# A decoder layer on eight cores: leaner opening loads, a later store of Q, two pairs of PSUM banks at the end of attention, and LayerNorm and up weights moved apart

## The chip, the cores and the metric

The kernel runs on the 8 cores of one Trainium2 chip, cores 0 to 3 on one die and 4 to 7 on the other. Every core computes 2048 of the 16384 tokens, and no core waits for another. The metric is the device time of the slowest core in microseconds (us).

Executions come in two states. In the fast one the cores have a granted TensorE clock of about 0.99. In the slow one a die, sometimes both, falls to between 0.81 and 0.98 and its cores take up to 19% longer.

## The reference, cut to what matters

```python
def token_mixer(x, w_in, b_in, sinks, g_mix_a, g_mix_b, w_out):
    proj = jnp.einsum('bsd,de->bse', x, w_in) + b_in
    # ... split into qa, ka, va (8 heads of 128) and qb, kb, vb (16 query heads of 64, 2 kv heads)
    qa = rope(qa, pos); ka = rope(ka, pos)
    ya = dilated_mixture_attention(qa, ka, va)     # patterns (128,1), (512,4), (2048,16)
    # ... rope on qb, kb
    yb = sink_window_attention(qb, kb, vb, sinks)
    y = jnp.concatenate([rms_norm(ya, g_mix_a), rms_norm(yb, g_mix_b)], axis=-1)
    return jnp.einsum('bse,ed->bsd', y, w_out)

def swiglu(x, w_up, w_down):
    gate, up = jnp.split(jnp.einsum('bsd,df->bsf', x, w_up), 2, axis=-1)
    return jnp.einsum('bsf,fd->bsd', jax.nn.silu(gate) * up, w_down)

x = layer_norm(ALPHA * x + token_mixer(...), ln1_g, ln1_b)
x = layer_norm(ALPHA * x + swiglu(x, w_up, w_down), ln2_g, ln2_b)
# D_MODEL 2048, SEQ 16384, D_FF 5632, group A 8 heads, group B 16 heads
```

## The kernel before

The large matmuls are bf16; a few small ones, for sums over partitions, are float32. Each core goes through these stages: V and K of its tokens and of the 2048 before them; Q and group B's attention; group A's attention; the output projection; LayerNorm 1 (LN1); and the feed-forward in two halves of 1024 tokens (`st` 0 and 1), with LN2 in the second half's shade. TensorE is fed by the other engines, and each engine's operations come in the order in which the program lists them for it (a case where that costs 1.1 us is shown below: an exponential behind a Square). The scheduling helpers `S_.pe`, `S_.act`, `S_.dve` and `S_.pool` record an operation with what it reads and what it writes. In the views of the profile PE is TensorE and PEld its weight loads; `arena` is the kernel's whole SBUF (the on-chip memory) and `sp` its PSUM (where TensorE writes its sums), used as eight banks.

The opening loads x and the V weights in turn, and the second token tile waits for the whole of its x:

```python
    for p_ in (1, 1, 2, 4, 4, 4):                      # x of the first tile and wv, in turn
        ...
        S_.dma("pool", wv[:, q_, :], k.wv_d[q_], ...)  # [128, 1152]: 1024 columns of A, 128 of B
    S_.dma("sp", bv, k.bv_d[0], [], [bbv], "bv")       # V's bias, already spread over 128 partitions
    load_x(1, (4, 4, 4, 4))
    ...
    load_ra(0); load_ra(1)                             # rotary tables
    # first tile: 8 matmuls (4 blocks x 2 banks) as each chunk lands; then
    for blk in range(4):
        v_tile(1, blk)                                 # waits for bx[1] + bwv, all chunks
```

Group A runs in 32 units (8 heads, 4 residues `c`), each with three patterns: S matmuls, an exponential on ScalarE (ACT), a mask on VectorE (DVE), and PV matmuls into one pair of banks, `ob` and `lb`. At the end of a unit the pair is evacuated. Until unit 25 each unit also computes a Q projection; `dveq` holds its rotary operations, of which the last, the add at L331, stores Q.

```python
    for u in range(32):
        for p_ in range(3):
            ... spend.append(a_S(hn, cn, pats[pn], nb % 2))   # S, exponential, mask of a later pattern
            run(dveq, 2 if p_ == 0 else 1)
            if p_ == 2:
                proj(u + 32 + LEAD, 0)
            a_PV(h, c, pats[p_], spend.pop(0), p_ == 0, p_ == 2)
        a_evac(h, c)

    def a_evac(h, c):
        S_.act(... Ln of lb ...); S_.act(... Exp ...)
        S_.dve(... yc = ob * ls ...)                   # L879: frees the banks
        S_.act(... sq = Square(yc) ...)                # L887, for group A's RMS norm
        S_.pool(... y = copy of yc ...)                # reordered, then stored when the head is done
        S_.pool(... acc += sq ...)
        if c == 3 and h < 7:
            S_.dma("sp", k.ys_d[h], y, ...)            # store of a head of y
```

y goes through HBM. Its loads for the output projection are issued from one queue, in this order: 14 for the first half, 14 for the second half, and then, in unit 28, head 6 of both halves, whose store has just been put into the same queue.

```python
    for c in KCB: y_load(0, c)
    for c in KCA[:6]: y_load(0, c)
    for c in KCB + KCA[:6]: y_load(1, c)
    ...
        if u == 28:
            k.y_load(0, 6); k.y_load(1, 6)
```

LN1 has its mean and inverse deviation in SBUF, and its sums on GpSimd (POOL):

```python
    def ln1_tile(st, n, hh, z, bz):
        S_.dve(... z = z - mu ...)                     # L1139
        S_.dve(... z = z * rs ...)                     # L1140
        S_.act(... x1b = z * g + b ...)
        S_.dma("act", k.x1s_d[n, :, c0:c0 + 512], z, ...)     # the residual, stored in HBM
    # the output projection's second half works these off as it goes:
        for _ in range(2 if si % 2 else 1):
            if jobs:
                jobs.pop(0)()
```

The softmax here doesn't subtract the row's maximum and nothing guards it: scores larger than these inputs give would overflow.

Of the kernel before, what the change touches and what calls it, by code (L numbers as in the profile page):

```python
# [203 lines left out]
def build(debug=False):  # L204
    nc = bass.Bass("TRN2", target_bir_lowering=False)
    dt = nc.dram_tensor
    k = K()
    k.nc = nc
    ein = lambda n, s: dt(n, s, F32, kind="ExternalInput").ap()
    k.xT_d = ein("xT", [8, 128, KC, 512])  # L210
    k.xres_d = ein("xres", [KC, 128, TOK])
    k.ropeA_d = ein("ropeA", [8, 128, 2, 512])
    k.ropeB_d = ein("ropeB", [4, 128, 2, 512])
    k.ropeBh_d = ein("ropeBh", [128, 2, 128])
    k.maskA1_d = ein("maskA1", [128, 4, 64])
    k.mask_d = ein("mask", [128, 3, 256])
    k.onh_d = ein("onh", [128, 128])
    k.perm_d = ein("perm", [128, 128])
    k.wv_d = ein("wv", [KC, 128, VW])
    k.wk_d = ein("wk", [8, 128, KC, 128])  # L220
    k.wkb_d = ein("wkb", [128, KC, 128])
    k.wq_d = ein("wq", [16, 128, KC, 128])
    k.bqk_d = ein("bqk", [128, 25])
    k.bsw_d = ein("bsw", [128, 16])
    k.bv_d = ein("bv", [2, 128, VW])
    k.wout_d = ein("wout", [KC, 128, KC, 128])
    k.wup_d = ein("wup", [FC, 128, KC, 256])
    k.wdn_d = ein("wdn", [KC, 128, FC, 128])
    k.gmix_d = ein("gmix", [128, KC])
    k.lnp_d = ein("lnp", [128, 4, KC])  # L230
    k.sinks_d = ein("sinks", [128, 8])
    k.outT_d = dt("outT", [KC, 128, TOK], F32, kind="ExternalOutput").ap()
    k.ka_d = dt("ka", [8, 8, 128, 512], BF16, kind="Internal").ap()
    k.kb_d = dt("kb", [128, NKB * 128], BF16, kind="Internal").ap()
    k.vs_d = dt("vs", [2 * TOK, VW], BF16, kind="Internal").ap()
    k.ys_d = dt("ys", [KC, 128, TOK], BF16, kind="Internal").ap()
    k.rb_d = dt("rb", [128, TOK], F32, kind="Internal").ap()
    k.wdb_d = dt("wdb", [KC, 128, FC, 128], BF16, kind="Internal").ap()
    k.x1s_d = dt("x1s", [KC, 128, TOK], F32, kind="Internal").ap()
    k.z2s_d = dt("z2s", [KC, 128, TOK], F32, kind="Internal").ap()  # L240

    stack = ExitStack()
    with stack:
        k.S = Sched(nc, stack)
        k.arena = stack.enter_context(nc.sbuf_tensor("arena", [128, ARENA_EL], BF16))
        k.SP = [stack.enter_context(nc.psum_tensor("sp%d" % i, [128, 1024], F32)) for i in range(4)]
        k.bBK = [Buf("bk%d" % i) for i in range(8)]
        persist(k)
        phase1(k)
        phase2(k)  # L250
        final = phase3(k)
        k.S.emit(final)
    return nc
# [30 lines left out]
def persist(k):  # L284
# [15 lines left out]
    S_.dma("pool", k.perm, k.perm_d, [], [k.bperm], "perm")  # L300
# [53 lines left out]
def phase1(k):  # L354
# [48 lines left out]

    s0 = xs[slot_of[0]]
    bl0 = []
    kc = 0
    for p_ in (1, 1, 2, 4, 4, 4):
        o_ = XO + kc * 1024
        b_ = S_.buf("x0_%d" % kc, o_, o_ + p_ * 1024)
        S_.dma("pool", s0[:, kc:kc + p_, :], k.xT_d[0, :, kc:kc + p_, :], [], [b_], "x0_%d" % kc)  # L410
        bl0 += [b_] * p_
        for q in range(kc, kc + p_, 2):
            n_ = min(2, kc + p_ - q)
            for q_ in range(q, q + n_):
                S_.dma("pool", wv[:, q_, :], k.wv_d[q_], [], [bwv[q_]], "wv%d" % q_)
        kc += p_
    bx[0] = bl0
    S_.dma("sp", bv, k.bv_d[0], [], [bbv], "bv")
# [6 lines left out]
    S_.dma("pool", wkb, k.wkb_d, [], [bwkb], "wkb")  # L425
    k.bvs, k.bka, k.bkb = [], [[] for _ in range(8)], []
# [5 lines left out]

    def v_out(t, blk, groups, banks):
        vi = nx("vo", 2)
        vo, bvo = VO[vi]
        w = 0
        for gi, (c0, c1) in enumerate(groups):
            bk = banks[gi]
            args = dict(out=vo[:, c0:c1], in0=bank(k, bk)[:, 0:c1 - c0], in1=bv[:, c0:c1], op=ALU.add)
            S_.dve(lambda args=args: nc.vector.tensor_tensor(**args), [k.bBK[bk], bbv],  # L440
                   [bvo] if gi == 0 else [], [] if gi == 0 else [bvo])
            w = c1
        b = Buf("vs%d_%d" % (t, blk))
        r0 = t * 512 + blk * 128
        S_.dma("sp", k.vs_d[r0:r0 + 128, 0:w], vo[:, 0:w], [bvo], [b], "vo%d" % vi)
        k.bvs.append(b)

    def v_tile(t, blk):
# [3 lines left out]
        for (c0, c1) in groups:  # L452
            bk = nx("bk", 8)
            banks.append(bk)

            def mm(bk=bk, c0=c0, c1=c1):
                for kc in range(KC):
                    ins = nc.tensor.matmul(bank(k, bk)[:, 0:c1 - c0], x[:, kc, blk * 128:blk * 128 + 128], wv[:, kc, c0:c1],  # L458
                                           start=(kc == 0), stop=(kc == KC - 1))
                return ins  # L460
            S_.pe(mm, bx[t] + bwv, [k.bBK[bk]])
        v_out(t, blk, groups, banks)

    def k_tile(t, h):
# [11 lines left out]
        ko, bko = KO[ki := nx("ko", 3)]  # L476
# [32 lines left out]
    load_ra(0)  # L509
    load_ra(1)  # L510
# [9 lines left out]
    for blk in range(4):  # L520
        v_out(0, blk, [(0, 512), (512, 1024)], [blk * 2, blk * 2 + 1])
    for blk in range(4):
        v_tile(1, blk)
# [37 lines left out]
def phase2(k):  # L561
# [33 lines left out]
    VA = [PW("vA0", 69 * 128), None]  # L595
# [17 lines left out]
    def load_kv(h):  # L613
        if h == 1:
            P2 = Place(k, o_b, 2 * ARENA_EL)
            KA[1] = P2("kA1", 8 * 512)
            VA[1] = P2("vA1", 69 * 128)
# [6 lines left out]
        first = [True]  # L624

        def ld(out, in_):
            S_.dma("sp", out, in_, k.bvs, [bv_] if first[0] else [], "va%d" % (h % 2), joins=[] if first[0] else [bv_])
            first[0] = False
        own = k.vs_d[TOK - 128:2 * TOK, col]
        ld(vt[:, 0:17, :], own.rearrange("(b p) d -> p b d", p=128))  # L630
        own2 = k.vs_d[TOK - 512:2 * TOK, col].rearrange("(j i c) d -> c i j d", c=4, i=128)
        for c in range(4):
            ld(vt[:, 17 + 5 * c:22 + 5 * c, :], own2[c])
        v3 = k.vs_d[:, col].rearrange("(f m r) d -> f m r d", f=2, r=16)
        for f in range(2):
            ld(vt[:, 37 + 16 * f:53 + 16 * f, :], v3[f])
# [198 lines left out]

    def a_PV(h, c, pat, pb, first, last):
        p = pb[0]
        vt, bv_ = VA[h % 2]
# [31 lines left out]
        S_.pe(mm, [pb[1], bv_, k.bones, k.bonh], [bOB, bLB])  # L870

    k.y7 = None

    def a_evac(h, c):
        ls, bls = LS[nx("ls", 2)]
# [8 lines left out]
        if h == 0:  # L884
            S_.pool(lambda: nc.gpsimd.tensor_tensor(out=ac, in0=yc, in1=yc, op=ALU.mult), [byc], [bacc[c]])
        else:
            S_.act(lambda: nc.scalar.activation(out=sq, in_=yc, func=AF.Square), [byc], [SQ[1]])  # L887
# [9 lines left out]
        if h > 0:  # L897
            eng, ve = ("dve", nc.vector) if (h, c) == (7, 3) else ("pool", nc.gpsimd)
            S_._add(eng, lambda: ve.tensor_tensor(out=ac, in0=ac, in1=sq, op=ALU.add), [SQ[1], bacc[c]], [bacc[c]])
        if c == 3 and h < 7:  # L900
# [6 lines left out]
    def reduce_a(c):  # L907

        bk = 6 + nx("pj", 2)
        if c == 3:  # L910
            bk = 4
# [41 lines left out]
    for u in range(32):  # L953
# [11 lines left out]
        for p_ in range(3):  # L965
# [4 lines left out]
            run(dveq, 2 if p_ == 0 else 1)  # L970
# [3 lines left out]
            if 28 <= u < 31:  # L974
                for _ in range(2):
                    if len(k.norms) > 48:
                        out_norm(k, *k.norms.pop(0))
            if u >= 29 and p_ == 1:
                reduce_a(u - 29)
        if u == 0:  # L980
            reduce_b(3)
        a_evac(h, c)
        proj(u + 32 + LEAD, 1)
    for i, (n, hh) in enumerate(OUT_PRE):
        out_mm(k, 0, n, hh, OUT_BK[i], KCB, True, False)
        if i == 2:
            reduce_a(3)
# [94 lines left out]
def phase3(k):  # L1082
# [53 lines left out]
    def ln1_tile(st, n, hh, z, bz):  # L1136

        (mu, bmu), (rs, brs) = stat[hh]
        S_.dve(lambda: nc.vector.tensor_tensor(out=z, in0=z, in1=mu, op=ALU.subtract), [bz, bmu], [bz])  # L1139
# [19 lines left out]

    for st in range(2):  # L1160
# [7 lines left out]

        def load_xr(si):
            if si < len(steps):  # L1170
                n, hh = steps[si]
                c0 = st * TS + hh * 512
                S_.dma("sp", xr[si % 4][0], k.xres_d[n, :, c0:c0 + 512], [], [xr[si % 4][1]], "xr")
        for si in range(3):
            load_xr(si)
        for si, (n, hh) in enumerate(steps):
            bk = OUT_BK[si % 6]
            load_xr(si + 3)
            xb, bxb = xr[si % 4]
# [9 lines left out]
            if si == 0:  # L1189
                while fins:  # L1190
                    fins.pop(0)()
# [5 lines left out]
            stats(n, hh, z, bz, sqs)  # L1197
            for _ in range(2 if si % 2 else 1):
                if jobs:
# [11 lines left out]
    wdone(k, "xr")  # L1211
    def ln2_tile(st, n, hh, idx):
        c0 = st * TS + hh * 512
        (mu, bmu), (rs, brs) = stat[hh]
        if st == 0:
            z, bz = slot("zl%d" % idx, R[0] + (4 + idx % 6) * 2048)
            S_.dma("sp", z, k.z2s_d[n, :, c0:c0 + 512], [bz2s[(n, hh)]], [bz], "zl%d" % (idx % 6))
# [52 lines left out]
    for st in range(2):  # L1270
        h = [None] * FC
        bh = [None] * FC
        order = [(0, 0), (1, 0), (0, 1), (1, 1)] + [(f, hh) for f in range(2, FC) for hh in range(2)]
        wcur = {}
        sg = [slot("sg%d_%d" % (st, i), misc(8 + i)) for i in range(2)]
        for ui, (f, hh) in enumerate(order):
# [22 lines left out]
            if ui == 0:  # L1299
                while fins:  # L1300
                    fins.pop(0)()
            for _ in range(2):
                if jobs:
# [5 lines left out]
        for si, (n, hh) in enumerate(steps):  # L1309
            wkey = ("d", st, n, hh if st else 0)  # L1310
            w, bw = k.wts[wkey]
            bk = si % 4
# [76 lines left out]
def prepare_inputs(x, w_in, b_in, sinks, g_mix_a, g_mix_b, w_out, ln1_g, ln1_b, w_up, w_down, ln2_g, ln2_b):  # L1389
# [13 lines left out]
    wv = con(np.concatenate([w_in[:, 2048:3072], w_in[:, 4224:4352]], 1).reshape(KC, 128, VW))  # L1403
# [22 lines left out]
    shared = dict(wq=wq, wk=wk, wkb=wkb, wv=wv, bqk=bqk, bsw=bsw, wout=wout, wup=wup, wdn=wdn, gmix=gmix, lnp=lnp,  # L1426
# [35 lines left out]
```

## Time and profile before

The median was 3120.53 us (3116.96 to 3122.29 fast, one slow at 3255.28).

The page's first part gives busy time, share of the span and instructions of each engine on the slowest core, core 4:

```profile
PE 2981.2 (96%) x15993; PEld 1425.5 (46%) x15993; DVE 1089.1 (35%) x1440; ACT 645.8 (21%) x891; POOL 608.3 (20%) x592
```

TensorE is busy 2981.2 of 3112.1 us. What can be won is its idle time of 131 us, and the slow clock after pauses: by the trace's records of the granted clock this core's TensorE was busy for 35.8 us at a clock of 0.50, the tail left out. The view of waits says what ended TensorE's pauses on core 4. Each line names the waiting instruction, what it waited for, the sum in us, how often, and the longest.

```profile
PE sp L849 <- DVE arena L879: 32.5, 26, 5.4
PE sp L516 <- DMA arena<-wv: 23.9, 7, 9.3
PE sp L458 <- DMA arena<-xT: 11.6, 1, 11.6
PE sp L1288 <- DMA arena<-wup: 6.0, 1, 6.0
...
PE sp L1076 <- DVE arena L1065: 2.5, 1, 2.5
```

The first line is PV waiting for the evacuation of the one pair of banks; the next two are the opening. The fourth is the first up weights (over all cores the waits for up weights are 4.7 us in the mean), and the last is the output projection waiting for the norm of y (L1065).

The timeline of TensorE in the opening (columns: start, duration, engine, line, operation, count; in brackets the idle time before and what ended it) shows the slow start (8 matmuls in 3.57 us, where K's first 15 take 3.40), the second tile's wait, and K's start at 96.82:

```profile
9.35 3.57 PE L516 MATMUL sp<-arena 128*128 128x512 bf16 x8 [9.35 <-DMA arena<-wv]
...
67.58 29.41 PE L458 MATMUL sp<-arena 128*128 128x512 bf16 x128 [11.60 <-DMA arena<-xT]
96.82 3.40 PE L471 MATMUL sp<-arena 128*128 128x512 bf16 x15
```

One end of a unit in group A, in the timeline of core 4:

```profile
809.48 1.04 DVE L331 TENSOR_TENSOR arena<-arena 128x512 bf16<-128x512 f32 x1
810.06 0.64 PE L824 MATMUL sp<-arena 128*128 128x64 bf16 x17
810.45 0.67 DVE L879 TENSOR_TENSOR arena<-sp,arena 128x512 bf16<-128x512 f32 x1
...
811.27 0.63 ACT L887 ACTIVATE arena<-arena 128x512 f32<-128x512 bf16 x1 [1.37 <-DVE arena L879]
811.81 2.12 ACT L829 ACTIVATE arena<-sp 128x1024 bf16<-128x1024 f32 x2
```

The evacuation (L879) begins as Q's store (L331) ends. Two lines further on the next exponential (L829) starts at 811.81; its scores were ready at 810.70 (S, L824: 810.06 plus 0.64).

LN1's two operations between 1095 and 1230 us, in the view of groups (busy us and mean ns of one; then idle before and what ended it):

```profile
L1140 DVE TENSOR_TENSOR arena<-arena 128x512 f32<-128x512 f32 x32 | 53.7, 1678 | 3.5 <-DVE arena L1139 0.2 <-ACT arena L1115 0.2
L1139 DVE TENSOR_TENSOR arena<-arena 128x512 f32<-128x512 f32 x32 | 26.2, 818 | 0.0
```

Both have two inputs in SBUF, and beside POOL's sums they slow down. Over all cores, the 160 of the first half's 256 multiplies (L1140) that began while a sum ran took 1.57 to 2.95 us, 2.25 in the mean; the other 96 took 0.69 to 0.91. The subtractions (L1139) took 1.12 us in the mean when they began during a sum (80 of them) and 0.68 otherwise. The residual add of the output projection (L1195), which has one input in PSUM, took 681 ns in the same stretch, and no more than 0.69 us where it began during a sum (1080 to 1260 us, all cores).

### The profile page before, as it was taken

The numbers are of one execution on the slowest core, as the hardware profiler recorded it, in microseconds if no ns is written. First come the engines' busy times: TensorE is split into PE (matmuls) and PEld (weight loads), VectorE is DVE, ScalarE is ACT, GpSimd is POOL, SyncE is SP. The second block draws the span as 40 slices with busy tenths as digits, with TensorE's granted clock in tenths as the row PEclk, the third lists the DMA queues.
The fourth block names the chain that finished last, engine by engine and source line by source line (L and its number), as shares of the span: only waits on it lengthen the run. The fifth ranks groups of instructions, "written<-read, shape, count | busy, mean of one in ns | idle before, by whom it ended". The sixth has DMA issues, their size and how long they took to land.

```text
span 3112.1 us, 40181 instructions; the slowest of 8 cores (3099.8 to 3112.1 us)
## 1 busy us (share of the span) xinstructions
PE 2981.2 (96%) x15993; PEld 1425.5 (46%) x15993; DVE 1089.1 (35%) x1440; ACT 645.8 (21%) x891; POOL 608.3 (20%) x592
## 2 busy tenths in 40 slices
PE   5999999998997998999999999999999999999996
PEld 2445554545664443444444444444444444444443
DVE  0555555787776776420010000001421000100123
ACT  0000000665555133320000001111320000001223
POOL 2000000452322877000000002222000000002234
PEclk9999999999999999999999999999999999999998
DMA  9852213155548798754434447888864344335554
GB/s 175 160 125 81 78 52 80 42 125 120 127 111 208 148 192 173 150 118 80 80 70 82 76 98 187 211 205 196 206 148 82 70 80 79 70 102 185 180 207 166
DMA packets 191032, 398.48 MB, mean 128 GB/s; under 512 B 86912, under 2 KB 104576, under 8 KB 169856
## 3 DMA queue, kind: packets, MB, share of 16 engines
q0 software_dynamic: 29232, 167.06, 31.2%
q1 hardware_dynamic: 144912, 198.44, 21.4%
q10 hardware_dynamic: 16704, 30.42, 2.7%
q8 instruction: 128, 2.10, 0.3%
q14 instruction: 56, 0.46, 0.1%
HBM read 471.11 MB, written 91.82 MB: 181 GB/s over the span
## 4 chain that ended last, share of the span: by engine, by line
PE 75%; DMA 11%; DVE 7%; issue 3%; ACT 3%; POOL 1%; another core or an unknown queue 0%; SPq 0%; DVEq 0%; ACTq 0%; POOLq 0%
PE sp L1288 37%; PE sp L1322 10%; PE sp L471 7%; DMA arena<-x1s 7%; PE sp L458 7%; PE sp L695 5%; PE sp L1076 4%; DMA arena<-wv 1%; DVE arena L658 1%; DMA arena<-z2s 1%; DVE arena L1140 1%; ACT arena L1317 1%; DVE arena L1333 1%; DVE arena L879 1%; ACT arena L829 1%
## 5 line engine op out<-in xcount | busy, mean ns | idle before, releaser
L1288 PE MATMUL sp<-arena 128*128 128x512 bf16 x5632 | 1220.4, 380 | 10.4 <-DMA arena<-wup 6.0
L1288 PEld LDWEIGHTS sp<-arena 128*128 128x128 bf16 x5632 | 552.0, 98 | 679.7 <-issue 18.5
L1322 PE MATMUL sp<-arena 128*128 128x512 bf16 x2816 | 608.3, 379 | 2.2 <-ACT arena L1295 2.2
L1296 DVE TENSOR_TENSOR arena<-sp,arena 128x512 bf16<-128x512 f32 x176 | 121.6, 692 | 983.9 <-ACT arena L1295 983.9
L1322 PEld LDWEIGHTS sp<-arena 128*128 128x128 bf16 x2816 | 275.4, 98 | 335.3 <-issue 3.7
L1295 ACT ACTIVATE arena<-sp 128x512 f32<-128x512 f32 x176 | 105.1, 598 | 928.0 <-PE sp L1288 919.9
L127 POOL DMA_DIRECT2D arena<-wup x88 | 46.7, 530 | 1102.7 <-PE sp L1288 1071.1
L1116 POOL TENSOR_TENSOR arena<-arena 128x512 f32<-128x512 f32 x119 | 160.6, 1349 | 435.5 <-DVE arena L1333 396.8
L695 PE MATMUL sp<-arena 128*128 128x512 bf16 x1024 | 237.0, 381 | 3.9 <-DVE arena L349 3.9
L1076 PE MATMUL sp<-arena 128*128 128x512 bf16 x1024 | 222.3, 379 | 5.7 <-DVE arena L1195 3.2
L1333 DVE SCALAR_TENSOR_TENSOR arena<-arena,sp 128x512 f32<-128x512 f32 x64 | 44.0, 688 | 520.6 <-ACT arena L1317 273.9
L458 PE MATMUL sp<-arena 128*128 128x384 bf16 (+1 forms) x1168 | 212.0, 344 | 11.6 <-DMA arena<-xT 11.6
L471 PE MATMUL sp<-arena 128*128 128x512 bf16 x1024 | 222.2, 379 | 0.0
L658 DVE TENSOR_TENSOR arena<-arena 128x1024 bf16<-128x1024 bf16 x160 | 143.9, 914 | 69.3 <-ACT arena L829 56.1
L1117 POOL TENSOR_TENSOR arena<-arena 128x512 f32<-128x512 f32 x119 | 164.6, 1384 | 0.0
L458 PEld LDWEIGHTS sp<-arena 128*128 128x128 bf16 x1168 | 114.5, 98 | 107.8 <-issue 14.3
L1076 PEld LDWEIGHTS sp<-arena 128*128 128x128 bf16 x1024 | 99.8, 98 | 128.3 <-issue 9.4
L471 PEld LDWEIGHTS sp<-arena 128*128 128x128 bf16 x1024 | 100.3, 98 | 120.2
L695 PEld LDWEIGHTS sp<-arena 128*128 128x128 bf16 x1024 | 96.9, 98 | 114.6 <-issue 9.5
L343 ACT ACTIVATE arena<-sp,arena 128x512 bf16<-128x512 f32 (+1 forms) x37 | 25.1, 679 | 564.2 <-PE sp L491 442.1
L1317 ACT ACTIVATE arena<-arena 128x512 f32<-128x512 f32 x64 | 52.0, 813 | 366.2 <-DMA arena<-x1s 365.7
L440 DVE TENSOR_TENSOR arena<-sp,arena 128x384 bf16<-128x384 f32 (+1 forms) x81 | 47.9, 605 | 199.9 <-PE sp L458 115.7
(118 smaller groups left out, 2047.3 us busy)
## 6 DMA issues: line engine op xcount, KB each, us to landing
arena<-wup POOLq DMA_DIRECT2D x88, 1024.0 KB, 8.9
arena<-wdb SPq DMA_DIRECT2D x32, 1408.0 KB, 6.7
arena<-wdn POOLq DMA_DIRECT2D x16, 1408.0 KB, 13.1
wdb<-arena SPq DMA_DIRECT2D x16, 1408.0 KB, 12.5
arena<-wout POOLq DMA_DIRECT2D x32, 512.0 KB, 10.3
arena<-xres SPq DMA_DIRECT2D x64, 256.0 KB, 7.9
x1s<-arena ACTq DMA_DIRECT2D x64, 256.0 KB, 7.5
arena<-x1s SPq DMA_DIRECT2D x64, 256.0 KB, 6.9
```

Of the source, the lines that this page charges most:

```text
L458: ins = nc.tensor.matmul(bank(k, bk)[:, 0:c1 - c0], x[:, kc, blk * 128:blk * 128 + 128], wv[:, kc, c0:c1], start=(kc == 0), stop=(kc == KC ...
L471: ins = nc.tensor.matmul(bank(k, bk), wk[h][:, kc, :], x[:, kc, :], start=(kc == 0), stop=(kc == KC - 1))
L658: S_.dve(lambda: nc.vector.tensor_tensor(out=pg, in0=pg, in1=m.to_broadcast([128, rows, 1024 // rows]), op=ALU.mult), [bp, b], [bp])
L695: ins = nc.tensor.matmul(bank(k, bk), w[:, kc, :], x[:, kc, :], start=(kc == 0), stop=(kc == KC - 1))
L1076: ins = nc.tensor.matmul(bank(k, bk), w[:, kc, :], y[:, kc, hh * 512:(hh + 1) * 512], start=(first and i == 0), stop=(last and i == len(kc ...
L1116: S_.pool(lambda: nc.gpsimd.tensor_tensor(out=za, in0=za, in1=z, op=ALU.add), [bz, bza], [bza])
L1117: S_.pool(lambda: nc.gpsimd.tensor_tensor(out=qa, in0=qa, in1=sq, op=ALU.add), [bsq, bqa], [bqa])
L1288: ins = nc.tensor.matmul(bank(k, a + half), w[:, kc, half * 128:half * 128 + 128], xb[:, kc, hh * 512:(hh + 1) * 512], start=(kc == 0), st ...
L1295: S_.act(lambda si=si, a=a: nc.scalar.activation(out=sg[si][0], in_=bank(k, a), func=AF.Silu), [k.bBK[a]], [sg[si][1]])
L1296: S_.dve(lambda si=si, a=a, f=f, hh=hh: nc.vector.tensor_tensor(out=h[f][:, hh * 512:(hh + 1) * 512], in0=bank(k, a + 1), in1=sg[si][0], o ...
L1317: S_.act(lambda xb=xb, n=n: nc.scalar.activation(out=xb, in_=xb, func=AF.Identity, bias=k.lnp[:, 1, n:n + 1], scale=k.lnp[:, 0, n:n + 1]), ...
L1322: ins = nc.tensor.matmul(bank(k, bk), w[:, fc, :], h[fc][:, hh * 512:(hh + 1) * 512], start=(fc == 0), stop=(fc == FC - 1))
```

## The change

The change has four parts. In the opening, only what the first V tile needs is loaded first: V's bias as one row that TensorE spreads over the partitions, group B's V weights and the rotary tables later, and the second tile in quarters over 8 banks. In group A, the add that stores Q comes after the evacuation, the Square after the next unit's first exponential, and a head's V is loaded in parts with a buffer each. From unit 28 on, two pairs of banks are used in turn, and the norms of y are spread one to each PV (cut below). In LN1 of the first half, mean and deviation are copied into PSUM, LN1's sums wait while the two finishing steps are spread out, and the up weights' place comes free earlier. The up stage's order and the down stage's banks change as well.

```diff
 # opening
-    S_.dma("sp", bv, k.bv_d[0], [], [bbv], "bv")
+    S_.dma("sp", bvr, k.bv_d[0][0:1], [], [bbvr], "bvr")
+    for g in range(3):
+        S_.pe(... matmul(bank(k, g)[:, 0:384], k.onesf[0:1, :], bvr[:, g * 384:(g + 1) * 384]) ...)
+        S_.act(... bv[:, g * 384:(g + 1) * 384] = copy of the bank ...)
-                S_.dma("pool", wv[:, q_, :], k.wv_d[q_], [], [bwv[q_]], "wv%d" % q_)
+            S_.dma("pool", wv[:, q, 0:1024], k.wv_d[q], [], [bwv[q]], "wv%d" % q)
+    S_.dma("pool", wv[:, :, 1024:1152], k.wvb_d, [], [bwvb], "wvb")      # after wk
+    def load_ra0(t):                                                     # after the second tile's x
+        S_.dma("sp", ra[t], k.ropeA_d[t], [bx[1][KC - 1]], [bra[t]], "ra%d" % t)
-    for blk in range(4):
-        v_tile(1, blk)
+    for kg in range(4):
+        for b in range(8):
+            ... four matmuls of quarter kg into bank b, waiting for bx[1][4 * kg] and its weights
 # ... (cut) V and K of the first tiles into buffers of their own
 # group A
-        S_.pe(mm, [pb[1], bv_, k.bones, k.bonh], [bOB, bLB])
+        S_.pe(mm, [pb[1], k.bones, k.bonh] + ([bv_[0]], [bv_[1 + c]], bv_[5:7])[pat], [bOB, bLB])
+    def o_banks(u):
+        i = 6 if u >= 28 and u % 2 == 0 else 4
+        return bank(k, i), k.bBK[i], bank(k, i + 1), k.bBK[i + 1]
-            run(dveq, 2 if p_ == 0 else 1)
+            if p_ == 0:
+                while sqq:
+                    sqq.pop(0)()                     # the Square of the unit before
+            run(dveq, (2, 1, 0)[p_])
...
         a_evac(h, c)
+        run(dveq, 1)                                 # Q's store
-        bk = 6 + nx("pj", 2)
-        if c == 3:
-            bk = 4
+        bk = (4, 6, 5, 4)[c]                         # banks of the RMS sums
 # LN1 and up
+        if st == 0:
+            for bk, (v, b) in ((4, stat[hh][0]), (5, stat[hh][1])):
+                if n == 0:
+                    S_.act(... bank(k, bk) = copy of v ...)
+            mu, rs, bmu, brs = bank(k, 4), bank(k, 5), k.bBK[4], k.bBK[5]
-            if si == 0:
-                while fins:
-                    fins.pop(0)()
+            if si >= 1 and fins:
+                fins.pop(0)()
+            if st == 1 and si == 27:
+                wdone(k, "xr")                       # the place for up weights comes free
-            stats(n, hh, z, bz, sqs)
+            todo.append((n, hh, z, bz, sqs))
+            while todo and not fins:
+                stats(*todo.pop(0))
-        order = [(0, 0), (1, 0), (0, 1), (1, 1)] + [(f, hh) for f in range(2, FC) for hh in range(2)]
+        order = [(f, hh) for f in range(FC) for hh in range(2)]
-            for _ in range(2):
+            for _ in range(2 - st):
-            bk = si % 4
+            bk = (2, 3, 4, 5, 0, 1)[si % 6]          # down stage
 # ... (cut) loads of LN2's residual ahead of use, residual buffers of the last four steps, host packing
```

## The prediction

> **What bounds it.** TensorE: 2981 of 3112 us busy (page, slowest core); a warm 128x512 matmul starts every 0.216 us. So the change can only win TensorE's idle time (131 us) and what its slow clock costs after pauses. The waits and windows views place the idle:
>
> - Opening, 0 to 97 us: two V tiles of 27.6 us each are done only at 97.0. The DMA engines are full (share 1.0). TensorE waits 23.9 us for wv and 11.6 us for the second x tile; its first matmuls run at half speed.
> - 500 to 560: 6.5 us. 690 to 740: 7.3 us.
> - Group A, 740 to 950: 16.2 us, nearly all PV behind the DVE evacuation: 0.6 us per unit, 1.3 at a head's last.
> - End of group A, 950 to 1010: 18 us; waits up to 3.8 us, slow matmuls after them.
> - Output projection, LN1, first up weights, 1110 to 1260: 13.8 us (wup 6.0 us).
> - Second up stage's start, 2150 to 2230: 5.5 us. Down starts: 1.1 us twice.
> - Tail after the last down matmul: 29 us.
>
> **Steps, costed.**
>
> 1. *Opening, -21 us.* Out of the first V tile's way go bv (0.59 MB), ropeA (1.05 MB) and a ninth of wv (1.05 MB). About 15.3 MB are read until wv's last piece lands at 50.6 us, some 318 GB/s; so 2.7 MB are 8.5 us. The second tile, in quarters over 8 banks, starts as its x lands, hiding the 11.6 us wait: first V ends near 47.5, K starts near 76 (was 97). Added: three small matmuls and ACT copies, hidden behind the first loads.
> 2. *Q's store behind the evacuation, -14 us.* The add that writes Q (1.04 us) ends at 810.5, just when the evacuation starts, though its exponential ended at 809.9. Taking it away lifts the evacuation 0.5 us, the size of the wait. A head's last wait is V landing: loads in parts, most needed first, remove it.
> 3. *Two bank pairs, -13 us.* The last units take 8.0 to 10.6 us; then ACT paces them (three exponentials of 1.02, Ln, Exp and Square of 0.6 each, sometimes 1.75 more): 5 to 7 us.
> 4. *LN and up weights, -20 us* with the slow clock after the pauses. DVE's two LN1 operations take 1.6 to 2.9 us beside POOL's sums, 0.69 alone; the pair of steps takes 9.0 us against 6.9 of matmuls. [...] mean and deviation in PSUM should make it 0.69. The contention is in this trace. wup, behind POOL's backlog, then comes in time.
>
> [...]
>
> Untouched: 500 to 560, 690 to 740, the tail. Sum -68; I allow for slippage.
>
> **Prediction:** 3054 us, 80% range 3038 to 3076. Faster by over 2%: 0.56; within 2%: 0.43; slower: 0.01.
>
> **Right or wrong.** K starts by 74 to 79 us; PV waits for evacuation in 740 to 950 (shifted) under 3 us; last four units under 26 us together (34 before, from 959.8 to 993.8); LN1's DVE operations at 0.7 us; no wait for wup; idle at the second up stage under 1.5 us; tail 29 us.
>
> **What would break it.** The opening's DMA rate falling; the evacuation still late because ACT is; a DMA-bound FFN start.

Two passages are cut from this text, as marked. No term of the sum falls with them: -21, -14, -13 and -20 still make the -68. What step 4 needs is measured: the 1.6 to 2.9 us are the multiply's beside POOL's sums, and an operation with one input in PSUM kept its 0.68 us there, as said above; that LN1's two operations would do the same was the author's estimate. In the opening, the half speed shows in groups of equal matmuls: 8 took 3.57 us at 9.35 and 3.45 at 16.50, 16 took 3.61 at 21.50. The DMA engines' share is 0.98 until 50.6 us and 1.01 until 97. The 318 GB/s, and so the 8.5 us, are an estimate: 15.3 MB, the float32 sizes in the program of the first tile's x, wv, bv and ropeA, over the 48 us between the first of these loads (2.27 us) and wv's last piece. The profile, which counts what was moved, has 165 GB/s for these 50.6 us.

## More of the kernel before

The queue of the y loads, in SyncE's timeline (SPq is its sequencer, and a group's duration is the time in which it issued them):

```profile
949.31 34.25 SPq L127 DMA_DIRECT2D arena<-ys  x28
983.66 0.81 SPq L127 DMA_DIRECT2D ys<-arena  x1
994.95 0.80 SPq L127 DMA_DIRECT2D arena<-ys  x2
```

The 28 loads hold the queue for 34 us. The store of head 6 comes out behind them, and its reload 11 us later, when the store has landed. The list of TensorE's waits above has only 2.5 us for it: the chain is nearly hidden.

## The result, and the profile after

The median is 3068.20 us (fast runs 3066.76, 3067.20 and 3069.21; one slow run at 3601.22 with die 1 at a clock of 0.82). Ratios in this document are the mean time of one kernel's fast runs over that of the other's of the same rounds, so not quite the ratio of the medians quoted. The ratio to the kernel before is 0.9833, interval 0.9810 to 0.9855: 1.7% faster, and within the 2% bound.

The page's first part, again for core 4:

```profile
PE 2964.0 (97%) x15721; PEld 1425.1 (46%) x15999; DVE 1057.6 (34%) x1440; ACT 656.0 (21%) x906; POOL 631.5 (21%) x593
```

TensorE's idle time fell from 131 to 104 us (3068.1 less 2964.0). Part of the rest of the gain is less slow clock: outside the tail, TensorE was busy at a granted clock of 0.50 for 37.2 us before and 15.1 after, in the mean of the cores, by the trace's clock records (they begin 12 to 28 us into the execution). Four cores of the kernel after also show 0.81, for 15.0 to 22.3 us. Some matmul records are missing (15721 where the weight loads count 15999), so the 2964.0 is a little low.

To see where the time went, I took the start of each stage's first matmul on every core from the trace, and averaged the differences over the 8 cores. The table's times are worked out in that way, in us.

| stage | before | after | difference | forecast |
|---|---|---|---|---|
| opening, until the first K | 97.6 | 77.2 | -20.4 | -21 |
| rest of V and K, Q's first projections, group B | 622.4 | 622.3 | 0 | 0 |
| group A, until the first output matmul | 268.8 | 250.6 | -18.2 | -27 (Q's store -14, bank pairs -13) |
| output projection and LN1, until the first up matmul | 238.8 | 243.3 | +4.5 | -20 for these three |
| first up stage | 620.1 | 613.8 | -6.3 | |
| down, second up, down | 1229.1 | 1221.1 | -8.0 | |
| tail | 30.2 | 29.3 | -0.9 | 0 |
| span | 3107.0 | 3057.6 | -49.5 | -68 |

The waits of TensorE on core 4 after the change:

```profile
PE sp L1130 <- DVE arena L1119: 11.2, 2, 10.7
PE sp L420 <- DMA arena<-bv: 10.3, 1, 10.3
PE sp L896 <- DVE arena L927: 8.8, 13, 3.5
PE sp L907 <- DVE arena L699: 7.5, 6, 2.1
PE sp L1130 <- DVE arena L1261: 5.8, 1, 5.8
...
PE sp L1366 <- DMA arena<-wup: 1.6, 1, 1.6
```

PV's wait for the evacuation (L896 for L927) fell from 32.5 to 8.8 us. The top line is the small one of before: the output projection's wait for the norm of y (L1119) grew from 2.5 to 11.2 us. Over all cores its mean is 7.8 us. Two more lines matter below: a mask (L699) that stands behind norms in DVE's order, 7.5 us where masks in group A had cost 1.5, and the residual add of the output projection (L1261). The add takes 5.8 us on this core and 1.8 in the mean of the cores; in the kernel before TensorE waited for it too, 3.2 us on every core.

The opening:

```profile
10.29 4.17 PE L420 MATMUL sp<-arena 1*128 1x384 f32 x6 [10.29 <-DMA arena<-bv]
15.40 32.99 PE L536 MATMUL sp<-arena 128*128 128x512 bf16 x126 [0.94 <-ACT arena L422]
49.62 27.79 PE L554 MATMUL sp<-arena 128*128 128x512 bf16 x125 [1.23 <-DVE arena L543]
77.25 43.11 PE L486 MATMUL sp<-arena 128*128 128x512 bf16 x195
```

The second tile starts 1.23 us after the first and then runs without a wait, and K starts at 77.25. The first V matmul starts 6 us later than before, at 15.40, since the small matmuls that spread the bias wait for its row. The first tile then finds nearly all of its loads landed: TensorE's waits for V's weights are 1.5 us in the mean of the cores, 21.9 before. This tile ends at 48.4 us (15.40 plus 32.99), 7.6 us earlier than before (67.58 less the wait of 11.60).

SyncE's queue at the end of group A:

```profile
922.10 35.38 SPq L127 DMA_DIRECT2D arena<-ys  x28
957.58 0.72 SPq L127 DMA_DIRECT2D ys<-arena  x1
969.52 0.80 SPq L127 DMA_DIRECT2D arena<-ys  x2
...
973.44 8.04 DVE L1119 SCALAR_TENSOR_TENSOR arena<-arena 128x512 bf16<-128x512 bf16 x12 [8.86 <-DMA arena<-ys]
975.00 25.35 PE L1130 MATMUL sp<-arena 128*128 128x512 bf16 x104 [10.65 <-DVE arena L1119]
```

The last two lines are DVE's and TensorE's of the same stretch. The chain is as long as before, while the units in front of it are 9 us shorter: the wait that was hidden is now in the open. After its pause of 10.65 us TensorE also runs slowly for 4.7 us: the weight loads from 974.97 to 979.65 came every 0.43 us, at a granted clock of 0.50, and the 95 after that in 20.42 us, 0.21 each, at 1.00.

LN1's operations, in the view of groups between 1095 and 1200 us:

```profile
L1199 DVE TENSOR_TENSOR arena<-arena,sp 128x512 f32<-128x512 f32 x32 | 22.0, 688 | 3.5 <-DVE arena L1198 0.3
L1198 DVE TENSOR_TENSOR arena<-arena,sp 128x512 f32<-128x512 f32 x32 | 21.8, 681 | 4.6 <-ACT sp L1196 4.6
L1261 DVE SCALAR_TENSOR_TENSOR arena<-arena,sp 128x512 f32<-128x512 f32 x26 | 17.8, 685 | 35.5 <-DMA x1s<-arena 18.0 <-DMA arena<-xres 9.8 <-PE sp L1130 7.7
```

The multiply went from 1678 to 688 ns and the subtraction from 818 to 681, as forecast. The third line has a new wait of DVE's: the residual add (L1261) waits 18.0 us for a store of LN1's output (x1s).

### The profile page after: what moved, and what is told of

It is laid out like the page before. It is cut to its first block, busy times and chain, and to the rows that moved or that the text cites. A ratio compares the mean times of both kernels' runs of the same rounds, so it can differ in the third digit from the quotient of the medians.

```text
span 3068.1 us, 39918 instructions; the slowest of 8 cores (3050.9 to 3068.1 us)
## 1 busy us (share of the span) xinstructions
PE 2964.0 (97%) x15721; PEld 1425.1 (46%) x15999; DVE 1057.6 (34%) x1440; ACT 656.0 (21%) x906; POOL 631.5 (21%) x593
## 3 DMA queue, kind: packets, MB, share of 16 engines
q1 hardware_dynamic: 144770, 197.86, 21.9%
## 4 chain that ended last, share of the span: by engine, by line
PE 91%; DMA 3%; ACT 2%; DVE 1%; SPq 1%; issue 1%; POOL 0%; DVEq 0%; ACTq 0%; POOLq 0%
PE sp L1366 39%; PE sp L1399 20%; PE sp L486 7%; PE sp L473 6%; PE sp L736 5%; PE sp L1130 5%; DMA x1s<-arena 2%; SPq L127 1%; PE sp L536 1%; PE sp L554 1%; PE sp L907 1%; DVE arena L927 1%; PE sp L795 1%; ACT arena L925 1%; PE sp L896 0%
## 5 line engine op out<-in xcount | busy, mean ns | idle before, releaser
L1366 PE MATMUL sp<-arena 128*128 128x512 bf16 x5519 | 1212.1, 379 | 11.2 <-DVE arena L1261 3.7
L1366 PEld LDWEIGHTS sp<-arena 128*128 128x128 bf16 x5632 | 551.3, 98 | 672.7 <-issue 10.6
L1399 PEld LDWEIGHTS sp<-arena 128*128 128x128 bf16 x2816 | 275.5, 98 | 332.6 <-issue 0.6
L1170 POOL TENSOR_TENSOR arena<-arena 128x512 f32<-128x512 f32 x119 | 157.5, 1324 | 447.9 <-DVE arena L1410 393.5
L1130 PE MATMUL sp<-arena 128*128 128x512 bf16 x1003 | 225.3, 384 | 18.2 <-DVE arena L1119 11.2
L473 PE MATMUL sp<-arena 128*128 128x384 bf16 (+1 forms) x1036 | 182.4, 337 | 0.4
L1130 PEld LDWEIGHTS sp<-arena 128*128 128x128 bf16 x1024 | 100.9, 99 | 143.3 <-issue 26.6
L1171 POOL TENSOR_TENSOR arena<-arena 128x512 f32<-128x512 f32 x119 | 160.3, 1347 | 1.1 <-ACT arena L1169 1.1
L486 PEld LDWEIGHTS sp<-arena 128*128 128x128 bf16 x1024 | 100.2, 98 | 120.3
L736 PEld LDWEIGHTS sp<-arena 128*128 128x128 bf16 x1024 | 96.8, 98 | 114.4 <-issue 9.2
L699 DVE TENSOR_TENSOR arena<-arena 128x1024 bf16<-128x1024 bf16 x160 | 141.3, 897 | 23.6 <-ACT arena L783 12.6
L473 PEld LDWEIGHTS sp<-arena 128*128 128x128 bf16 x1040 | 101.7, 98 | 79.6
L1394 ACT ACTIVATE arena<-arena 128x512 f32<-128x512 f32 x64 | 52.0, 813 | 394.9 <-DMA arena<-x1s 393.9
L343 ACT ACTIVATE arena<-sp,arena 128x512 bf16<-128x512 f32 (+1 forms) x37 | 25.1, 678 | 505.3 <-PE sp L510 383.1
L1169 ACT ACTIVATE arena<-arena 128x512 f32<-128x512 f32 x119 | 74.9, 630 | 201.6 <-DVE arena L1261 71.2
## 6 DMA issues: line engine op xcount, KB each, us to landing
arena<-wout POOLq DMA_DIRECT2D x32, 512.0 KB, 10.7
arena<-xres SPq DMA_DIRECT2D x64, 256.0 KB, 8.6
x1s<-arena ACTq DMA_DIRECT2D x64, 256.0 KB, 8.1
arena<-x1s SPq DMA_DIRECT2D x64, 256.0 KB, 7.8
```

The costliest lines, as they stand in the source:

```text
L473: ins = nc.tensor.matmul(bank(k, bk)[:, 0:c1 - c0], x[:, kc, blk * 128:blk * 128 + 128], wv[:, kc, c0:c1], start=(kc == 0), stop=(kc == KC ...
L486: ins = nc.tensor.matmul(bank(k, bk), wk[h][:, kc, :], x[:, kc, :], start=(kc == 0), stop=(kc == KC - 1))
L699: S_.dve(lambda: nc.vector.tensor_tensor(out=pg, in0=pg, in1=m.to_broadcast([128, rows, 1024 // rows]), op=ALU.mult), [bp, b], [bp])
L736: ins = nc.tensor.matmul(bank(k, bk), w[:, kc, :], x[:, kc, :], start=(kc == 0), stop=(kc == KC - 1))
L1130: ins = nc.tensor.matmul(bank(k, bk), w[:, kc, :], y[:, kc, hh * 512:(hh + 1) * 512], start=(first and i == 0), stop=(last and i == len(kc ...
L1170: S_.pool(lambda: nc.gpsimd.tensor_tensor(out=za, in0=za, in1=z, op=ALU.add), [bz, bza], [bza])
```

## The experiments

All twelve runs are of the kernel after with one edit or a few, in three batches, each on one chip with the kernel before beside it. The fast runs of the kernel before took 3114.05 to 3115.47 us in the first batch (and one 3139.77), 3115.06 to 3118.09 in the second, and mostly 3111.76 to 3115.46 in the third (fast ones also at 3124.84 and 3141.29). Intervals are wide, and differences under 1% are read from the stages of fast profiles (means of 8 cores), as in the table above. There is one profile of each run. Two profiles of the same kernel (the first and the repeat below) agree to 1.1 us in every stage and to 2.1 us in the span; the cores of one profile lie further apart (236.5 to 248.2 us in the output stage of the repeat).

Two theories stood against each other for the output stage. One says that the y queue causes the loss: the norm waits for head 6's reload, which the bank pairs brought into the open. Its rival says that the slow stage comes from LN1's part of the change. For group A's gain, the theory of the prediction was the place of Q's store; the rival is that something else made the evacuation early. The expectations number the theories; the text around each says in words what it tested.

### Repeat of the kernel after

There is no edit.

> The changed kernel once more, as the base line of this batch. Both theories: 0.983 of the kernel before; from the first output matmul to the first up matmul some 243 us (mean of the cores), of which 6 to 11 us are one wait for the norm of a y chunk.

Its fast runs took 3062.48 and 3061.35 us, the ratio is 0.9803 (0.9698 to 0.9907). The stages: opening 76.3, group A 251.1, output 242.2, first up 612.9, span 3055.5. This is the yardstick for the other runs.

### The y loads of the second half after head 6

```diff
     for c in KCA[:6]: y_load(0, c)
-    for c in KCB + KCA[:6]: y_load(1, c)
...
         if u == 28:
             k.y_load(0, 6)
-            k.y_load(1, 6)
+            for cy in KCB + KCA[:7]: k.y_load(1, cy)
```

> The changed kernel, but the 14 loads of y for the second half are issued behind the last store and reload of head 6 instead of ahead of it. Theory 1 (the faster end of group A only meets a chain of transfers that was hidden before: 28 loads in a row on one queue, then the store of head 6, then its reload, then its norm): the norm wait of 6 to 11 us falls under 2.5 us, the output stage shortens by 5 to 8 us, the run by 5 to 8 us (0.2%). Rival 1 (DVE is late with the norms as it has too much to do there): the wait stays over 5 us and the time does not move.

SyncE's queue on core 4 then reads:

```profile
918.48 8.09 SPq L127 DMA_DIRECT2D arena<-ys  x14
929.03 0.32 SPq L127 DMA_DIRECT2D ys<-arena  x1
943.03 11.53 SPq L127 DMA_DIRECT2D arena<-ys  x16
```

The store of head 6 comes out at 929.03, and the reload at 943.03, 26 us earlier than in the kernel after. The 14 loads took 0.58 us each to issue, where the 28 in a row of the kernel after took 1.26 each. The norm's wait fell to 2.3 us, on every core alike, from a mean of 8.5 in the repeat (7.8 in the first profile). On core 4:

```profile
PE sp L1129 <- DVE arena L1118: 2.3, 2, 1.7
```

The output stage fell from 242.2 to 235.0, and the span from 3055.5 to 3048.6. The fast runs took 3054.23 to 3058.89 us, ratio 0.9784 (0.9713 to 0.9856). So the theory of the y queue holds for 7 us of the output stage; the first up stage and all later ones are unchanged (613.0 against 612.9 for the former).

### One bank pair in group A's end: two tries with a wrong result, two right ones

The edit is run with the queue as it is, and together with the early reload's edit above.

```diff
-        i = 6 if u >= 28 and u % 2 == 0 else 4
+        i = 4
```

> The changed kernel with one pair of output banks to the end of group A. Theory 1: the last units get slower by some 8 us, but the reload of head 6 arrives when it did, so the norm wait shrinks and the run loses under 4 us. Rival 1: the run loses all of the 8 us or more.

> Both edits. Theory 1: with the reload out of the way the two pairs are worth their full gain, so this run is 7 to 11 us slower than the run with the early store and reload alone, against under 4 us between the other two. Rival 1: the two pairs are worth the same with and without the early reload.

Both gave a wrong result (relative error 0.0447): the RMS sum of residue 0 still went to bank 4, in which, with one pair, a unit's output was being added up. That is a fault of my edit. The mend is one more line:

```diff
-        bk = (4, 6, 5, 4)[c]
+        bk = (6, 7, 5, 4)[c]
```

> One pair of output banks again, now with the two sums that fall inside the last units in banks 6 and 7, so that the result is right (the first try put one of them into the bank in which the output was being summed, and gave a wrong result). Theory 1: group A some 5.5 us longer than in the changed kernel (251), the output stage some 5 us shorter (242), sum under 3 us. Rival 1: group A longer by 5.5 us and the output stage unchanged.

> The same with the early store and reload of head 6. Theory 1: group A some 5 us longer, the output stage as short as with two pairs (235), so the pairs are now worth 4 to 6 us. Rival 1: as much as without the early reload.

These two are correct. The first one's profile fell in the slow state on die 1, so cores 0 to 3, at a clock of 0.99, are compared with the same cores of the repeat. The 2 x 2 table has group A, the output stage and the span.

| | two pairs | one pair | pairs are worth |
|---|---|---|---|
| head 6 behind 28 loads (cores 0 to 3) | 250.9, 243.4, 3057.2 | 258.6, 234.2, 3055.3 | -7.7, +9.2, span +1.9 |
| head 6 early (8 cores) | 252.0, 235.0, 3048.6 | 256.6, 235.0, 3054.0 | -4.6, 0, span -5.4 |

The wrong-result runs agree in size: with the queue as it was, group A 256.9, output 237.2 and span 3058.3, against 3055.5 for the repeat. With the queue as in the kernel after, the pairs shorten group A by 6 to 8 us and the output stage gives back 5 to 9, so their net worth lies between -3 and +2 us: nothing that can be told from zero. With head 6 early, they are worth 5.4 us. The run times say the same at their resolution: with head 6 early, 3054.23 to 3058.89 us with two pairs and 3061.41 to 3065.30 with one, on two chips on which the fast runs of the kernel before had medians of 3115.4 and 3115.8. The ratio is 0.983 for both kernels with one pair (intervals 0.9812 to 0.9847 and 0.9814 to 0.9846).

### LN1's mean and deviation back in SBUF

```diff
-        if st == 0:
+        if False:
             ...                                  # the copies into banks 4 and 5
-            mu, rs, bmu, brs = bank(k, 4), bank(k, 5), k.bBK[4], k.bBK[5]
+            pass
```

> The changed kernel, with mean and deviation of the first half read from SBUF again. Theory 2: the two DVE operations go from 0.69 back to 1.6 us and more beside POOL, but as transfers bound this stage the output stage moves by under 2 us. Rival 2b (DVE bounds the stage, as forecast): it gets longer by 3 to 6 us.

The groups between 1095 and 1230 us:

```profile
L1199 DVE TENSOR_TENSOR arena<-arena 128x512 f32<-128x512 f32 x31 | 52.2, 1684 | 3.2
L1198 DVE TENSOR_TENSOR arena<-arena 128x512 f32<-128x512 f32 x30 | 25.8, 861 | 0.0
```

With both inputs in SBUF the operations have the times of the kernel before. The output stage took 256.0 us (242.2 in the repeat), the wait for the up weights rose to 9.2 us and that for the residual add to 9.4. The fast runs took 3071.65 to 3077.65 us (and one 3103.82), ratio 0.9889 (0.9839 to 0.9938). So the copies into PSUM are worth 13.8 us in the kernel after. The theory that expected under 2 us fell, and its rival, with 3 to 6, was too small. It also follows that the new order with the old operations is worse than the old order: 256.0 against 238.8 us. The late reload explains some 7 of these 17 us; the rest I have not taken apart. The add's wait for an x1s store was 1.7 to 11.3 us by core in this run, against 10.4 to 18.0 in the kernel after.

### Other places for LN1's buffers

In the kernel after, the residual add of step 15 writes into a place that job 16 still stores from, and the last four residual buffers lie in places that the last stores still read. This edit gives both other places.

```diff
-    zbase = [12, 0]
+    zslot = [list(range(12, 44)), list(range(12)) + [12 + i for i in
+             (0, 1, 2, 6, 8, 10, 12, 14, 16, 18, 3, 4, 5, 7, 9, 11, 13, 15, 17, 19)]]
-            o = o_h + (zbase[st] + si) * 2048
+            o = o_h + zslot[st][si] * 2048
-                    xr.append(slot("xrz%d" % si, o_h + (si + 12) * 2048))
+                    xr.append(slot("xrz%d" % si, o_h + (32 + 2 * (si - 28)) * 2048))
```

> The changed kernel, with the places of the second half's z chosen so that each one's earlier owner was normalized and stored long before, and the four late residual buffers as well. Theory 2 (the output projection's second half waits for places whose owner's store has not landed): the DVE wait of 10 to 18 us for an x1s store at step 15, and the last wait of 10 to 16 us for a residual, fall under 5 us; TensorE's waits for DVE there (0 to 6 us) and for the first up weights (0 to 6 us) fall under 1.5 us; output and first up stages together shorter by 4 to 7 us. Rival 2 (the DMA engines are full there, whatever the places): the waits move to other transfers and the stages do not get shorter by over 2 us.

The residual add's group on core 4, between 1095 and 1230 us:

```profile
L1261 DVE SCALAR_TENSOR_TENSOR arena<-arena,sp 128x512 f32<-128x512 f32 x26 | 17.9, 687 | 30.4 <-PE sp L1130 16.3 <-DMA arena<-xres 13.3 <-ACT arena L1169 0.7
```

The wait for x1s is gone, on every core. TensorE's wait for the residual add in the output projection went from 1.2 us in the repeat (up to 3.9 by core; 1.8 in the first profile) to none. The output stage took 238.1 us (242.2) and the span 3049.9 (3055.5); the fast runs took 3055.65 and 3057.32. The wait for the up weights fell only from 3.2 to 2.6 us in the mean, where I had expected less.

Not all of the 4.1 us can be put down to these buffers. The wait for the norm, which comes before they are used, was also shorter here (6.9 us against 8.5), and the run with Q's store moved back, below, has an output stage of 237.9 us without this edit. With the reload early in both, the other places (together with the bias row's earlier load) are worth 2.1 us of the output stage (232.9 against 235.0) and 1.4 of the first up stage. So the buffers cost 2 to 4 us; only the add's wait of 1.2 us is shown directly.

### The finishing steps of LN1's sums at once, as before

```diff
-            if si >= 1 and fins:
-                fins.pop(0)()
+            if si == 0:
+                while fins:
+                    fins.pop(0)()
```

> The changed kernel, with both sums of LN1's first half again at the second half's first step, so that normalizing begins three steps earlier. Theory 3 (the later begin is what makes step 15 wait for an x1s store, which cost the output stage what the PSUM operands had won): the DVE wait for that store falls from 10 to 18 us to under 6 us, TensorE waits 2 us more at the sums, and the output and first up stages together are 1 to 5 us shorter. Rival 3: the wait stays and the stages are 2 us longer.

The output stage took 240.6 us and the span 3052.7, 1.6 and 2.8 us less than in the repeat, hardly more than two profiles of one kernel differ. The wait for x1s at step 15 stayed, 11.1 to 15.8 us by core (10.4 to 18.0 in the kernel after, 6.8 to 16.4 in the repeat), and the rival's 2 us more did not come either. The mechanism that I had put up, that the late sums delay the jobs and so the stores, is not what holds step 15 up. Only two runs of five are fast (3065.42 and 3083.62).

### Q's store back before the evacuation

```diff
-            run(dveq, (2, 1, 0)[p_])
+            run(dveq, (2, 1, 1)[p_])
...
         a_evac(h, c)
-        run(dveq, 1)
```

> The changed kernel, with the store of Q again in front of the evacuation. If Q's store is what held the evacuation, the cycle of a unit goes from 7.85 to 8.2 or 8.3 us and group A gets 7 to 10 us longer. If the moved squares or the parts of V did it, under 3 us.

Group A took 249.2 us, against 251.1 in the repeat: undoing this step cost nothing, and may have won 2 us. The span was 3050.6, the fast runs 3058.74 to 3063.39, ratio 0.9814 (0.9767 to 0.9861). The output stage was shorter too, 237.9 us against 242.2, with a wait for the norm of 5.2 us against 8.5; why, I have not taken apart. For group A the timeline of core 4 says why:

```profile
790.51 1.04 DVE L331 TENSOR_TENSOR arena<-arena 128x512 bf16<-128x512 f32 x1
...
792.32 0.69 DVE L927 TENSOR_TENSOR arena<-sp,arena 128x512 bf16<-128x512 f32 x1 [0.77 <-ACT arena L925]
...
793.11 1.02 ACT L870 ACTIVATE arena<-sp 128x1024 bf16<-128x1024 f32 x1 [0.89 <-PE sp L865]
793.15 1.39 POOL L936 COPY arena<-arena 128x512 bf16<-128x512 bf16 x1 [4.42 <-DVE arena L927]
...
794.03 0.62 ACT L946 ACTIVATE arena<-arena 128x512 f32<-128x512 bf16 x1
```

Q's store (L331) stands before the evacuation (L927) and is over at 791.55. DVE then waits 0.77 us for ACT's exponential (L925), so the store is in nobody's way. The next unit's first exponential (L870) comes right after its scores at 793.11, and the Square (L946) after it. In the kernel before it was the other way round: the Square held that exponential up by 1.1 us, from 810.70, when its scores were ready (S, L824: 810.06 plus 0.64), to 811.81. The same place in the repeat, with Q's store behind the evacuation:

```profile
790.80 0.69 DVE L927 TENSOR_TENSOR arena<-sp,arena 128x512 bf16<-128x512 f32 x1 [1.12 <-ACT arena L925]
791.41 1.03 DVE L331 TENSOR_TENSOR arena<-arena 128x512 bf16<-128x512 f32 x1
...
791.63 2.06 POOL L936 COPY arena<-arena 128x512 bf16<-128x512 bf16 x1 [3.82 <-DVE arena L927]
```

Here the store runs beside POOL's copy, which takes 2.06 us instead of 1.39, and the mask after it took 1.28 us instead of 0.69. That holds for the whole of group A: between 740 and 920 us, over all cores, POOL's copy took 2.05 us in the mean in the repeat and 1.39 with the store in front, and the masks 0.88 and 0.70 us. So, once the Square is out of the way, the moved store buys contention for no gain. What moving the store alone would have done in the kernel before, where it did stand directly before the evacuation, was not run.

### The opening's second tile as a whole

```diff
-    for kg in range(4):
-        for b in range(8):
-            ... quarter kg into bank b
     for blk in range(4):
-        v_out(1, blk, [(0, 512), (512, 1024)], [blk * 2, blk * 2 + 1])
+        v_tile(1, blk)
```

> The changed kernel, with the second V tile in the old order: one token block after another, each over all of x, so that it starts only when the whole second x tile has landed. As forecast, the opening's 20 us are two halves: fewer bytes ahead of the first tile (some 8 us) and the start by quarters (some 12 us). So here the first K tile starts 9 to 12 us later than in the changed kernel (76.3), near 87, and the run is that much longer. Rival (the bytes alone did it): under 3 us.

The profile is slow on die 1, so cores 0 to 3 count for the start of K (two of them had 0.98 over the whole run): 87.5, 86.6, 88.1 and 87.5 us, mean 87.4. In the repeat they were 77.8, 76.2, 75.5 and 76.1, mean 76.4. So the quarters are worth 11 us, which leaves 10 of the 21 for the rest of the opening's change, the bytes above all; no run put the bytes back alone. TensorE's opening on core 4 has the old wait back. (Its die is the slow one, but K starts there at 87.77, as on the others.)

```profile
57.55 30.39 PE L473 MATMUL sp<-arena 128*128 128x512 bf16 x128 [11.16 <-DMA arena<-xT]
87.77 12.46 PE L486 MATMUL sp<-arena 128*128 128x512 bf16 x57
```

The fast runs took 3069.62 and 3072.33 us (and one 3098.57), ratio 0.9875 (0.9813 to 0.9937).

### All that helped in one kernel

This has the early reload of head 6, the other places for LN1's buffers, and the bias row's load as the very first one.

```diff
+    S_.dma("sp", k.bvr, k.bv_d[0][0:1], [], [k.bbvr], "bvr")     # now ahead of the small loads
     for v, d in ((k.bqk, k.bqk_d), ...):
-    S_.act(... esink = Exp(esink) ...); S_.dve(... gmix *= 32 ...)   # these two now after the bias's copies
 # ... and the edits of the early reload and of the other places, as above
```

> The changed kernel with three mends: the early store and reload of head 6, the chosen places of z, and the row of bv loaded ahead of all small loads with the sinks' exponential behind bv's copies. Stage by stage: first K tile near 75 (76.3 in the changed kernel), output stage near 232 (242), first up stage near 612, the rest the same: some 14 us below the changed kernel, 3048 to 3056 by the clock of the runs, 0.979 of the kernel before, so faster than both.

The runs took 3051.09, 3051.81, 3051.94 and 3054.77 us, with one fast run at 3071.68 with two cores of die 1 at a clock of 0.98, and one slow run. The ratio to the kernel before is 0.9798 (0.9757 to 0.9839), which straddles the 2% bound. The mean span is 3044.8, 10.7 us below the repeat; I had expected 14. The output stage took 232.9 us and the first up stage 611.6, as expected. The bias row's part was a miss. TensorE waited 2.8 us for the row instead of 10, and V's first matmul started at 8.61 us (core 7, the slowest); but it then waited 8.5 us for V's weights in the mean of the cores, and K still started at 76.5. The opening is held by the loads, not by the bias. It is the fastest kernel of this study, about 0.35% below the kernel after by the spans (3044.8 over 3055.5), though on a different chip.

## Why the prediction was right or wrong

The time lies inside the range (3038 to 3076), 14 us above the centre of 3054. But the outcome held to be likeliest, faster by over 2% at 0.56, did not come: it was 1.7%. Point by point:

1. **The opening: right.** The forecast was -21 us with K at 76; it was -20.4, with K at 77.2. The split into about 8.5 us of bytes and the rest for the quarters fits: undoing the quarters alone cost 11 us, and the first V tile ended at 48.4 us on core 4, where 47.5 was forecast. The bytes were not undone alone. "Added: three small matmuls and ACT copies, hidden behind the first loads" holds for K's start, since moving the row forward didn't bring K forward. It doesn't hold for the first V matmul, which came 6 us later.

2. **Q's store: the step that failed.** The prediction said "Taking it away lifts the evacuation 0.5 us, the size of the wait". The evacuation did begin as the store ended (810.45 and 810.52), and that was read as the cause of the unit's length. But undoing just that step left group A as fast (249.2 against 251.1 us), where the expectation had it 7 to 10 us longer: with the rest of the change in place, DVE is done with the store 0.77 us before the evacuation can start, and then waits for ACT, which the prediction had named under "What would break it". I think that ACT's Square, by holding the next exponential up by 1.1 us, made DVE's masks and adds late from unit to unit, and that the moved Square gave the gain. The traces show the Square in front of that exponential before, and behind it in both kernels with the Square moved, but the rest is argued: no run moved the Square alone, or the store alone. Nor did a run load V in one part again. The profile only shows that the wait at a head's end went from between 1.24 and 1.35 us (0.96 at the first) to at most 0.43. The size was also too large: 24 units of core 4, the third to the 26th, took 199.9 us (744.88 to 944.79) and then 191.6 (722.32 to 913.96). That is 8.3 us, where 14 were forecast. The shortest units took 7.85 us in both kernels; 24 such units are 188.4, so at that pace 11.5 us were there to be won. The check "PV waits for evacuation in 740 to 950 (shifted) under 3 us" failed too, narrowly: over the same units core 4 has 3.5 us (717 to 920 us), 14.5 before, and 5.3 with the unit after them.

3. **The two bank pairs: right in kind, half in size, then given back.** In group A the experiments put them at 4.6 and 7.7 us, where 13 were forecast. With the whole change the last four units took 25.1 us (926.50 to 951.58) against the forecast of under 26 and 34.0 before. "Then ACT paces them" is not what the trace shows: in those 25.1 us ACT was busy for 19.0 and DVE for 23.6, and TensorE waited for masks, 5.3 us between 930 and 990, and those stood behind norms in DVE's order. What the prediction did not follow was the next thing to arrive. The reload of head 6 stood behind 28 loads in one queue. Before, it arrived just in time for the slow units; now it came after them. With the queue unchanged, the pairs were worth nothing that can be told from zero; with the reload early, they were worth 5.4 us.

4. **LN1 and the up weights: the mechanism right, the sum wrong by half.** LN1's operations came to 0.68 and 0.69 us as forecast, and the experiment puts the PSUM copies at 13.8 us in the new order. The forecast was -20 us for three stages together. They gave +4.5, -6.3 and -8.0, together -9.8. Two losses make up most or all of the gap. The late reload cost 7.2 us in the output stage; that belongs to point 3's change but fell here. The buffers cost 2 to 4 us: a faster LN1 issues its stores closer together (the first ten of x1s within 16.2 us on core 4, within 25.1 before), and step 15's add waits for one of them (18.0 us of DVE's time on core 4, 10.4 to 18.0 by core). Without these two, the three stages would be at -19 to -21; in the kernel with all that helped, where both are mended, they are at -22.8 (2065.2 against 2088.0). In the profile of before the add had no wait for x1s at all, though TensorE waited 3.2 us for the add there. The -6.3 and -8.0 of the later stages are read from the table: TensorE's waits there fell from 4.0 to 0.8 and from 5.9 to 0.2 us in the mean of the cores, but no run undid the changes to these stages. "wup … then comes in time" failed: the wait was 3.3 us in the mean (4.7 before). The second up stage's idle time was under 1.5 us, as forecast: none.

5. **The rest: right.** The tail is 29.3 us (30.2), and the stages between the opening and group A are the same to 0.1 us.

The profile of before held a sign of point 3: a 34 us queue with a small, urgent store at its end, and a wait of 2.5 us on it. Such a wait is nearly hidden, and shortening what hides it by 9 us brings most of that into the open.

## What to carry to other kernels

Before counting a gain from shortening a stage, look at every load that the next stage waits for, and at how much slack it has: a transfer just in time is the new bottleneck (here a wait of 2.5 us became 11.2). When an operation seems to hold another up because one ends as the other begins, look at what made the first one late, and undo one part alone before you believe it. When an engine gets faster, its stores can come closer together (here ten within 16.2 us, 25.1 before), so give the buffers that they free some distance.
